# A two-layer encoder trunk: the second dense block's sum and the late gathers put behind the next layer's first two normalisations

## Chip, cores, metric

One core of a Trainium2 chip. The metric is the device time of one execution in microseconds, median of three runs.

## What is computed

512 tokens of width 1024 pass two layers. A layer normalises and modulates, mixes (three kinds of attention, one projection in and one out), adds and normalises, and then sums for every token the 128 experts that its router chose out of 16384 (8 heads, 16 each). The cut that matters:

```python
x = _layer_norm(DEEPNORM_ALPHA * x + (1.0 + g1) * mix, ln1_g[l], ln1_b[l])
h = _modulate(x, sh2, sc2)
u = jnp.take(u_tab, eb, axis=0)
act = jax.nn.gelu(jnp.einsum('tkd,td->tk', u, hb), approximate=False)
vv = jnp.take(v_tab, eb, axis=0)
ffn = jnp.einsum('tk,tkd->td', gb * act, vv)
x = _layer_norm(DEEPNORM_ALPHA * x + (1.0 + g2) * ffn, ln2_g[l], ln2_b[l])
```

The next layer reads that x, so its first normalisation of a token block needs the finished sum of the block.

## The kernel before

The tokens are four blocks of 128 rows, xs[0] to xs[3]. The expert sums are done in two ways at the same time. Blocks 1 and 2 (DENSE) are done by matmul against all experts: `dense` runs 128 tiles of 128 experts, and for each it transposes and splits a tile of u, multiplies, and adds a tile of v into four PSUM banks `acc`. Blocks 0 and 3 are done by gathers: `experts` is a generator with one step for each gathered tile, 32 of u and then 32 of v in turn, 512 steps in all. A step has an indirect DMA on GpSimd's queue into one of the four buffers of `g`, and one VectorE instruction on it: a dot product for u (line 691), a weighted sum for v (line 706). So a buffer of `g` is used again only when VectorE has taken the gather that was in it.

`pace(ex, mark, n)` draws n steps of that generator and ties their VectorE instructions behind the instruction `mark`. Most steps are drawn beside the dense tiles. In layer 0 the last 50 (LATE[0]) are drawn when layer 1 has opened its pools (`late()`), with the mark at the end of block 1's `finish`. These are the last 18 u-gathers and the last 32 v-gathers of block 3, and `finish` of block 3 stands behind them. In layer 1 nothing is late (LATE[1] is 0).

`finish` (line 716) ends a block: it multiplies the sum by the gate row, adds alpha times x (line 718), and normalises into xs (`moments`, `affine`). The rows (gate, gain, bias) are spread over the partitions by a small matmul into a PSUM bank (`row_op`, line 220), in two halves, and VectorE reads the bank (lines 223 and 225). The two dense blocks take those banks from `ut()`, a pair of buffers in the dense loop's own pool. Block 0's and block 3's `finish` take them from `psx`, a pool with one buffer (tile name prow, tag ex). A sum of the dense blocks is copied by ScalarE from PSUM to a tile `fa` in the dense loop's SBUF pool.

Layer 1 begins with `open_attention`, whose pools lie where the dense loop's pools were: what is first written there waits until the dense loop's last use. `layer_setup` then loads small vectors over SyncE's queue, and `prepare` (line 351) normalises xs[0] and xs[1] into `ytok` (line 246), transposes and modulates them into hT. `project` multiplies both with w_in (line 154), `attend` and `output` do block 0, `between` adds and normalises, `queries` does the router's matmul. The order on each engine comes from a scheduler that works from priorities and a simulated timeline, so a change in program order can move instructions that the diff doesn't name.

Of the kernel before, what the change touches and what calls it, by code (L numbers as in the profile page):

```python
# [11 lines left out]
F32 = mybir.dt.float32  # L12
# [5 lines left out]
OP = mybir.AluOpType  # L18
# [3 lines left out]
P = 128  # L22
D = 1024
# [13 lines left out]
LATE = (50, 0)  # L37
# [15 lines left out]
def body(ctx, tc, x, c, positions, ada_w, ada_b, w_in, q_norm_g, kv_norm_g, w_uq, w_ukv, conv_w,  # L53
         w_o, ln1_g, ln1_b, peer_wq, peer_k1, peer_k2, peer_u, peer_v, ln2_g, ln2_b, out):
    nc = tc.nc
# [4 lines left out]
    pw = ctx.enter_context(tc.tile_pool(name="pw", bufs=1))  # L60
    gath = ctx.enter_context(tc.tile_pool(name="gath", bufs=4))
# [181 lines left out]

    def normalize(dst, src):
        mean, r = moments(src)
        nc.vector.tensor_scalar(dst, src, mean, r, op0=OP.subtract, op1=OP.mult)

    def affine(y, dst, tmp, src, ig, ib, mk=None, pool=None):
        mean, r = moments(src, pool)
# [101 lines left out]
    def prepare(y, b):  # L351
        hT = A.work.tile([P, KT, P], F32, name="hT", bufs=2)
        yt = A.work.tile([P, D], F32, name="ytok", bufs=1)
        normalize(yt, xs[b])
        transpose_cols(hT, yt, KT, scale=y.sc1, bias=y.sh1)
        y.hT[b] = hT

    def project(y, blocks, behind=None):
        l = y.l
# [313 lines left out]
    def experts(y, b, eidx, gw):  # L673
        def after(inst):
            if gate[0] is not None:
                tc.add_manual_dep(inst.ins, gate[0].ins.name,
                                  mybir.DependencyInfo(mybir.DependencyClass.NoSync, mybir.DependencyReason.DATA),
                                  reason="expert sums in pace with the dense tiles")

        h2 = pw.tile([P, D], F32, name="h2")  # L680
        nc.sync.dma_start(h2, h2tok[y.l][b // 2])
        acc = pw.tile([P, D], F32, name="acc")
        dots = pw.tile([P, PH, TOPK], F32, name="dots", bufs=1)
        wts = pw.tile([P, PH, TOPK], F32, name="wts", bufs=1)
        for h0 in range(0, PH, HB):
            slots = [(h, k) for h in range(h0, h0 + HB) for k in range(TOPK)]
            for j, (h, k) in enumerate(slots):
                g = gath.tile([P, D], F32, name="g")
                nc.gpsimd.indirect_dma_start(out=g, out_offset=None, in_=u_flat,  # L689
                                             in_offset=bass.IndirectOffsetOnAxis(ap=eidx[:, h, k:k + 1], axis=0))  # L690
                after(nc.vector.scalar_tensor_tensor(out=g, in0=g, scalar=1.0, in1=h2, op0=OP.mult, op1=OP.mult,  # L691
                                                     accum_out=dots[:, h, k:k + 1]))
                yield
            hs = slice(h0, h0 + HB)
            ge = nc.scalar.activation(wts[:, hs, :], dots[:, hs, :], AF.Gelu)
            if b == 0 and h0 < 2:
                exp_ln(ge)
            nc.vector.tensor_tensor(wts[:, hs, :], wts[:, hs, :], gw[:, hs, :], op=OP.mult)
            for j, (h, k) in enumerate(slots):
                g = gath.tile([P, D], F32, name="g")  # L700
                nc.gpsimd.indirect_dma_start(out=g, out_offset=None, in_=v_flat,  # L701
                                             in_offset=bass.IndirectOffsetOnAxis(ap=eidx[:, h, k:k + 1], axis=0))
                if h == 0 and k == 0:
                    r = nc.vector.tensor_scalar(acc, g, wts[:, h, k:k + 1], None, op0=OP.mult)
                else:
                    r = nc.vector.scalar_tensor_tensor(out=acc, in0=g, scalar=wts[:, h, k:k + 1], in1=acc,  # L706
                                                       op0=OP.mult, op1=OP.add)
                after(r)
                if h < PH - 1 or k < TOPK - 1:
                    yield  # L710
        tc.cur_priority -= 1000000
        finish(y, b, acc, lambda: psx.tile([P, 512], F32, name="prow", tag="ex"), pw)
        tc.cur_priority += 1000000
        yield
# [9 lines left out]
    def dense(y, blocks, res):  # L724
# [148 lines left out]
                yield held[0]  # L873
        fas = []
        for i in range(2):
            fa = dw.tile([P, D], F32, name="fa", tag="v", bufs=2)
            for g in range(2):
                nc.scalar.copy(fa[:, g * 512:(g + 1) * 512], acc[i][g])
            fas.append(fa)
        for b, fa in zip(blocks, fas):  # L880
            r = finish(y, b, fa, ut, dw)
            if b == min(blocks):
                held[0] = r
        st.close()
        yield held[0]

    def pace(ex, mark, n):
        gate[0] = mark
        for _ in range(n):
            next(ex)  # L890

    ada_first(range(4))
    for l in range(L):
        if l:
            open_attention(l)
            late()
        y = layer_setup(l)

        def pick(b, v1, fi):
            return topk(l, v1, fi, b, b not in DENSE)  # L900

        res = [None] * NB
        for b in (0, 1):
            prepare(y, b)
        layer_keys(y)
        ps = project(y, (0, 1))
        if l + 1 < L:
            ada_side(0, range(4, 12))
        layer_rows(y)
        behind = None  # L910
        for p in ps:
            b = p[0]
            attend(y, *p)
            if b == 1:
                for b2 in (2, 3):
                    prepare(y, b2)
            h = between(y, b, output(y, b, p[2]))
            r = queries(y, *h, range(4))
            if b == 0:
                behind = r  # L920
            res[b] = pick(b, *h[1:])
        p2, p3 = project(y, (2, 3), behind)
        if l + 1 < L:
            ada_side(1, range(12))
        attend(y, *p2)
        h = between(y, 2, output(y, 2, p2[2]))
        queries(y, *h, range(2))
        attend(y, *p3)
        rt = output(y, 3, p3[2])
        queries(y, *h, range(2, 4))  # L930
        res[2] = pick(2, *h[1:])
        h = between(y, 3, rt, lambda: A.ps.tile([P, 512], F32, name="prow", tag="at", bufs=2))
        queries(y, *h, range(4))
        res[3] = partial(pick, 3, *h[1:])
        A.stack.close()
        dn = dense(y, DENSE, res)
        ex = chain.from_iterable(experts(y, b, *res[b]) for b in range(NB) if b not in DENSE)
        pace(ex, None, EARLY[l])
        groups = 2 * P // TG
        for _ in range(groups):  # L940
            mark = next(dn)
            pace(ex, mark, 1)
        with tc.issue_after(mark.ins):
            res[3] = res[3]()
        n = 2 * 2 * NSLOT - EARLY[l] - LATE[l] - groups
        for a, mark in enumerate(dn):
            if a < NK:
                pace(ex, mark, (a + 1) * n // NK - a * n // NK)
        late = partial(pace, ex, mark, LATE[l])
        if not l + 1 < L:  # L950
            late()


_INS = ["x", "c", "positions", "ada_w", "ada_b", "w_in", "q_norm_g", "kv_norm_g", "w_uq", "w_ukv", "conv_w",
# [19 lines left out]
```

## Time and profile before

| | us |
|---|---|
| median of three runs (lowest, highest) | 3543.99 (3531.81, 3545.16) |
| the profiled execution | 3547.72 |
| its span, first to last instruction | 3546.0 |
| TensorE busy in the span | 3074.8 (87%) |
| VectorE | 2754.8 (78%) |
| GpSimd | 1456.3 (41%) |
| ScalarE | 928.7 (26%) |

Layer 0 ends and layer 1 begins at about 1770 to 1820 us of the span. Times of the rows below are from the span's start. A busy share is an average over stages with different limits, so the stretches around the change are read one by one.

### The profile page before, as it was taken

The page shows a single profiled execution, that of the slowest core. Times are in us where ns is not written, and L with a number is a line of the kernel's source. Part 1 is how long each engine was busy: PE and PEld are TensorE (multiplying, and loading weights), DVE is VectorE, ACT ScalarE, POOL GpSimd, SP SyncE. Part 2 cuts the span into 40 slices and gives each one's busy share as a digit, 9 for nine tenths or more (in the row PEclk, how much of TensorE's full clock was granted, in tenths as well). Part 3 has the DMA queues.
Part 4 walks back from the last instruction along what each step waited for, and adds up shares of the span by engine and source line. Part 5 has one row for each costly group of instructions (what it writes and reads, how often), then busy time and mean ns, then how long its engine had stood idle before and what let it go on. Part 6 is the DMA issues. An engine that isn't in the chain of part 4 may idle for free.

```text
span 3546.0 us, 51872 instructions
## 1 busy us (share of the span) xinstructions
PE 3074.8 (87%) x18364; PEld 2019.4 (57%) x18364; DVE 2754.8 (78%) x6213; ACT 928.7 (26%) x1859; POOL 1456.3 (41%) x1347
## 2 busy tenths in 40 slices
PE   7878879659999999999948987785789999999998
PEld 2433434436777777777724444444567767677775
DVE  3667897999777877677675578889998887776777
ACT  2342432222222222222222223312222222222221
POOL 1034563256433434444451144534454444434443
PEclk9989989859999999999969997896799999999998
DMA  8767968558888888899885577794779988889997
GB/s 290 239 206 256 329 227 305 173 192 289 301 325 304 314 308 320 305 343 350 330 296 198 171 273 259 261 325 155 245 275 344 338 309 318 314 323 335 361 352 255
DMA packets 340051, 1011.98 MB, mean 285 GB/s; under 512 B 40504, under 2 KB 53064, under 8 KB 339792
## 3 DMA queue, kind: packets, MB, share of 16 engines
q0 software_dynamic: 147456, 536.94, 42.5%
q1 hardware_dynamic: 192336, 471.73, 38.2%
q8 instruction: 146, 2.39, 0.3%
q14 instruction: 113, 0.93, 0.1%
HBM read 1002.06 MB, written 6.34 MB: 284 GB/s over the span
## 4 chain that ended last, share of the span: by engine, by line
PE 15%; DVE 12%; DMA 10%; issue 9%; POOL 3%; ACT 1%; DVEq 0%; POOLq 0%; ACTq 0%
DMA g<-in_peer_v,eidx 5%; PE acc L842 4%; PE pm L154 3%; DMA g<-in_peer_u,eidx 3%; DVE g L691 2%; DVE acc L706 2%; POOL g L689 2%; PE sp L824 1%; PE sp L825 1%; PE sp L826 1%; DVE tk_ef L661 1%; PE utp L810 1%; POOL g L701 1%; DVE o L790 1%; DVE o L781 1%
## 5 line engine op out<-in xcount | busy, mean ns | idle before, releaser
L701 POOL DMA_INDIRECT g<-in_peer_v,eidx x512 | 613.7, 1199 | 802.2 <-DVE acc L706 486.4
L842 PE MATMUL acc<-v,ge 128*128 128x512 f32 x2048 | 927.1, 595 | 6.8 <-DVE ge L830 6.7
L689 POOL DMA_INDIRECT g<-in_peer_u,eidx x512 | 593.0, 1158 | 755.8 <-DVE g L691 508.5
L706 DVE SCALAR_TENSOR_TENSOR acc<-g,wts,acc 128x1024 f32<-128x1024 f32 x508 | 668.8, 1316 | 143.0 <-DMA g<-in_peer_v,eidx 139.6
L691 DVE SCALAR_TENSOR_TENSOR g<-g,h 128x1024 f32<-128x1024 f32 x512 | 619.7, 1225 | 180.8 <-DMA g<-in_peer_u,eidx 180.2
L824 PE MATMUL sp<-hh,uh 128*128 128x256 f32 x2048 | 613.7, 300 | 1.1 <-ACT ge L828 1.1
L826 PE MATMUL sp<-hh,ul 128*128 128x256 f32 x2048 | 595.0, 291 | 0.0
L825 PE MATMUL sp<-hl,uh 128*128 128x256 f32 x2048 | 584.5, 285 | 0.0
L842 PEld LDWEIGHTS acc<-v,ge 128*128 128x128 f32 x2048 | 370.1, 190 | 372.0 <-issue 364.3
L812 ACT CAST uh<-utp 128x512 fp32r<-128x512 f32 x512 | 303.3, 594 | 911.7 <-PE utp L810 772.6
L814 DVE TENSOR_TENSOR ul<-utp,uh 128x512 fp32r<-128x512 f32 x512 | 346.5, 684 | 106.9 <-ACT uh L812 106.4
L824 PEld LDWEIGHTS sp<-hh,uh 128*128 128x128 f32 x2048 | 392.9, 192 | 6.1 <-issue 4.1
L825 PEld LDWEIGHTS sp<-hl,uh 128*128 128x128 f32 x2048 | 393.1, 192 | 4.6 <-issue 4.5
L826 PEld LDWEIGHTS sp<-hh,ul 128*128 128x128 f32 x2048 | 391.9, 191 | 0.1
L810 PE MATMUL utp<-ident,u 128*128 128x128 f32 x2048 | 304.9, 278 | 57.0 <-DVE ul L814 54.0
L810 PEld LDWEIGHTS utp<-ident,u 128*128 128x128 f32 x2048 | 237.4, 142 | 136.0 <-issue 66.4
L799 ACT COPY G<-pg 128x344 f32<-128x344 f32 (+1 forms) x192 | 146.4, 763 | 561.8 <-PE pg L797 557.9
L797 PE MATMUL pg<-o,o 128*128 128x43 bf16 (+1 forms) x4608 | 182.5, 190 | 97.7 <-DVE o L790 85.4
L797 PEld LDWEIGHTS <-o 128*128 128x128 bf16 x4608 | 162.6, 102 | 179.9 <-issue 84.5
L154 PE MATMUL pm<-wt,hT 128*128 128x512 f32 (+1 forms) x512 | 231.3, 601 | 24.2 <-DMA wt<-in_w_in 13.4
L154 PE MATMUL pm<-wt,h2T 128*128 128x512 f32 x512 | 238.2, 611 | 8.8 <-DMA wt<-in_peer_wq 8.2
L660 POOL TENSOR_TENSOR tk_pick<-tk_hot,tk_ce 128x400 f32<-128x400 bf16 x128 | 125.7, 982 | 153.6 <-DVE tk_hot L658 151.7
(234 smaller groups left out, 3259.9 us busy)
## 6 DMA issues: line engine op xcount, KB each, us to landing
u<-in_peer_u SPq DMA_DIRECT2D x256, 512.0 KB
v<-in_peer_v SPq DMA_DIRECT2D x256, 512.0 KB
wt<-in_peer_wq SPq DMA_DIRECT2D x128, 512.0 KB
adw<-in_ada_w SPq DMA_DIRECT2D x160, 256.0 KB
wt<-in_w_o SPq DMA_DIRECT2D x64, 512.0 KB
wt<-in_w_in SPq DMA_DIRECT2D x48, 512.0 KB
wt<-in_ada_w SPq DMA_DIRECT2D x16, 512.0 KB
g<-in_peer_u,eidx POOLq DMA_INDIRECT x512, 7.0
```

Of the source, the lines that this page charges most:

```text
L154: r = nc.tensor.matmul(pm[:, :n], lhsT=lhsT[:, k0 + k, :], rhs=wt[:, k, :n], start=k0 + k == 0, stop=k0 + k == KT - 1)
L689: nc.gpsimd.indirect_dma_start(out=g, out_offset=None, in_=u_flat, in_offset=bass.IndirectOffsetOnAxis(ap=eidx[:, h, k:k + 1], axis=0))
L691: after(nc.vector.scalar_tensor_tensor(out=g, in0=g, scalar=1.0, in1=h2, op0=OP.mult, op1=OP.mult, accum_out=dots[:, h, k:k + 1]))
L701: nc.gpsimd.indirect_dma_start(out=g, out_offset=None, in_=v_flat, in_offset=bass.IndirectOffsetOnAxis(ap=eidx[:, h, k:k + 1], axis=0))
L706: r = nc.vector.scalar_tensor_tensor(out=acc, in0=g, scalar=wts[:, h, k:k + 1], in1=acc, op0=OP.mult, op1=OP.add)
L797: nc.tensor.matmul(pg[:, tt, 0:n], lhsT=o2[:, tt // TI, :, tt % TI], rhs=o1a[:, tt // TI, p, 0:n, tt % TI], start=tt == 0 and p == 0, stop ...
L810: nc.tensor.transpose(pt[:, j * P:(j + 1) * P], u[:, k * P:(k + 1) * P], ident)
L814: nc.vector.tensor_tensor(ul.rearrange("p j t -> p (j t)"), pt, uh.rearrange("p j t -> p (j t)").bitcast(F32), op=OP.subtract)
L824: nc.tensor.matmul(sp, lhsT=uh[:, j, :], rhs=hh[:, k, :], start=k == 0, stop=False)
L825: nc.tensor.matmul(sp, lhsT=uh[:, j, :], rhs=hl[:, k, :], start=False, stop=False)
L826: nc.tensor.matmul(sp, lhsT=ul[:, j, :], rhs=hh[:, k, :], start=False, stop=k == KT - 1)
L842: nc.tensor.matmul(acc[i][g], lhsT=w[:, i * P:(i + 1) * P], rhs=v[:, g * 512:(g + 1) * 512], start=a == 0, stop=a == NK - 1)
```

## The change

`dense` finishes only block 1. Block 2's `fa` is put into a buffer of the gathers' ring (tag g), and its `finish` becomes a call that is made later, with the one-buffer pool `psx` and the small tiles of `pw` in place of the dense loop's own. In layer 1's beginning the order of the program is now: prepare blocks 0 and 1, finish block 2 of layer 0, draw the 50 late steps with the mark at block 1's normalisation (the instruction that writes `ytok`). At the end of layer 1 the same call is made after the last dense tile, and `pace` draws none.

```diff
     def prepare(y, b):
...
-        normalize(yt, xs[b])
+        r = normalize(yt, xs[b])
...
+        return r
...
         fas = []
         for i in range(2):
-            fa = dw.tile([P, D], F32, name="fa", tag="v", bufs=2)
+            if i:
+                fa = gath.tile([P, D], F32, name="fa", tag="g")
+            else:
+                fa = dw.tile([P, D], F32, name="fa", tag="v", bufs=2)
...
-        for b, fa in zip(blocks, fas):
-            r = finish(y, b, fa, ut, dw)
-            if b == min(blocks):
-                held[0] = r
+        held[0] = finish(y, blocks[0], fas[0], ut, dw)
+        rest.append(lambda: finish(y, blocks[1], fas[1], lambda: psx.tile([P, 512], F32, name="prow", tag="ex"), pw))
...
         if l:
             open_attention(l)
-            late()
...
         for b in (0, 1):
-            prepare(y, b)
+            r = prepare(y, b)
+        if l:
+            rest.pop()()
+            pace(ex, r, LATE[l - 1])
...
-        late = partial(pace, ex, mark, LATE[l])
         if not l + 1 < L:
-            late()
+            pace(ex, mark, LATE[l])
+            rest.pop()()
```

The order on the engines, at three places. In the names xs_95 to xs_98 are blocks 0 to 3, `g,dots<-g,h` is a u-gather's product, `acc<-g,wts,acc` a v-gather's, utp is a bank of the dense loop's pair, prow one of the pool with one buffer.

VectorE where layer 0 ends, from the end of block 1 to the first write of `ytok`, before:

```order
L225 SCALAR_TENSOR_TENSOR xs_96<-fa,rs_r,utp 128x512 x2
L691 SCALAR_TENSOR_TENSOR g,dots<-g,h_10865 128x1024 x4
L223 TENSOR_TENSOR fa<-fa,utp 128x512 x2
L691 SCALAR_TENSOR_TENSOR g,dots<-g,h_10865 128x1024
L718 SCALAR_TENSOR_TENSOR fa<-xs_97,fa 128x1024
...
L225 SCALAR_TENSOR_TENSOR xs_97<-fa,rs_r,utp 128x512 x2
L691 SCALAR_TENSOR_TENSOR g,dots<-g,h_10865 128x1024 x2
L298 MEMSET sqT 128x1024
...
L691 SCALAR_TENSOR_TENSOR g,dots<-g,h_10865 128x1024
L246 TENSOR_SCALAR ytok<-xs_95,bnmv,rs_r 128x1024
```

and with the change:

```order
L225 SCALAR_TENSOR_TENSOR xs_96<-fa,rs_r,utp 128x512
L225 SCALAR_TENSOR_TENSOR fa<-fa,bnmv,prow 128x512
L225 SCALAR_TENSOR_TENSOR xs_96<-fa,rs_r,utp 128x512
L225 SCALAR_TENSOR_TENSOR fa<-fa,bnmv,prow 128x512
L298 MEMSET sqT 128x1024
...
L225 SCALAR_TENSOR_TENSOR xs_97<-fa,rs_r,prow 128x512
L246 TENSOR_SCALAR ytok<-xs_95,bnmv,rs_r 128x1024
L246 TENSOR_SCALAR ytok<-xs_96,bnmv,rs_r 128x1024
L692 SCALAR_TENSOR_TENSOR g,dots<-g,h_10865 128x1024 x3
L325 CAST rows_160<-rf 32x256
```

Block 2's `finish` runs between block 1's instructions, and the 18 u-products that stood before `ytok` now stand behind it. On GpSimd's queue the first gather that is not yet issued then now stands behind the small instructions of both normalisations and the nine that make the masks; on SyncE's queue no row moves.

VectorE in layer 1's attention of block 0, from the last `ktok` of the projection to the masked scores `sbe`, before:

```order
L477 COPY ktok<-kr 128x8x32
L223 TENSOR_TENSOR acc<-acc,prow 128x512
L718 SCALAR_TENSOR_TENSOR acc<-xs_98,acc 128x1024
L237 BN_STATS bnst<-acc 128x6 x2
L499 TENSOR_REDUCE mx<-sc 128x4
...
L539 SCALAR_TENSOR_TENSOR sp_17102<-z,sbe 128x512
L541 SCALAR_TENSOR_TENSOR sp_17102<-ntri,sp_17102 128x512
L548 SCALAR_TENSOR_TENSOR sbe<-ntri,z 128x512
```

and with the change:

```order
L478 COPY ktok<-kr 128x8x32
L707 SCALAR_TENSOR_TENSOR acc<-g,wts,acc 128x1024
L500 TENSOR_REDUCE mx<-sc 128x4
L707 SCALAR_TENSOR_TENSOR acc<-g,wts,acc 128x1024
L500 TENSOR_REDUCE mx<-sc 128x4
...
L540 SCALAR_TENSOR_TENSOR sp_17102<-z,sbe 128x512
L707 SCALAR_TENSOR_TENSOR acc<-g,wts,acc 128x1024
L542 SCALAR_TENSOR_TENSOR sp_17102<-ntri,sp_17102 128x512
L707 SCALAR_TENSOR_TENSOR acc<-g,wts,acc 128x1024 x5
L549 SCALAR_TENSOR_TENSOR sbe<-ntri,z 128x512
L707 SCALAR_TENSOR_TENSOR acc<-g,wts,acc 128x1024
```

Block 3's `finish` stood here; now 17 v-products stand between the attention's own instructions (16 of them before `sbe`), and the `finish` comes behind them, beside `between` of block 0.

VectorE at the program's end, before (first fence) and with the change (second):

```order
L239 BN_AGGR bnmv<-bnst 128x2
L223 TENSOR_TENSOR fa<-fa,utp 128x512
L225 SCALAR_TENSOR_TENSOR acc<-acc,bnmv,prow 128x512
L223 TENSOR_TENSOR fa<-fa,utp 128x512
L718 SCALAR_TENSOR_TENSOR fa<-xs_97,fa 128x1024
L225 SCALAR_TENSOR_TENSOR acc<-acc,bnmv,prow 128x512
L237 BN_STATS bnst<-fa 128x6 x2
L225 SCALAR_TENSOR_TENSOR xs_98<-acc,rs_r,prow 128x512
```

```order
L239 BN_AGGR bnmv<-bnst 128x2
L225 SCALAR_TENSOR_TENSOR acc<-acc,bnmv,prow 128x512 x2
L225 SCALAR_TENSOR_TENSOR xs_98<-acc,rs_r,prow 128x512 x2
L223 TENSOR_TENSOR fa<-fa,prow 128x512 x2
L719 SCALAR_TENSOR_TENSOR fa<-xs_97,fa 128x1024
L237 BN_STATS bnst<-fa 128x6 x2
L239 BN_AGGR bnmv<-bnst 128x2
L225 SCALAR_TENSOR_TENSOR fa<-fa,bnmv,prow 128x512 x2
L225 SCALAR_TENSOR_TENSOR xs_97<-fa,rs_r,prow 128x512 x2
```

Blocks 3 and 2 took turns there, with banks of their own; now block 2 follows block 3, and both use the one prow bank.

## Rows read from the trace of the kernel before

**Rows 1.** The page: its span, and the group of the v-gathers' products

```profile
span 3546.0 us, 51872 instructions
...
L706 DVE SCALAR_TENSOR_TENSOR acc<-g,wts,acc 128x1024 f32<-128x1024 f32 x508 | 668.8, 1316 | 143.0 <-DMA g<-in_peer_v,eidx 139.6
```

**Rows 2.** Busy time by stretch: end of layer 0, start of layer 1, the program's end

```profile
core 0: us, PE busy (x) PEld busy (x) DVE busy (x) ACT busy (x) POOL busy (x), PEclk, DMA share, GB/s
1771.00:1803.00 32.00, 7.92 (x27) 3.13 (x25) 27.27 (x46) 2.25 (x4) 18.45 (x18) 0.58 0.64 215
1803.00:1822.00 19.00, 1.94 (x9) 1.60 (x9) 14.60 (x26) 8.62 (x12) 14.14 (x21) 0.50 0.95 283
1822.00:1912.00 90.00, 76.99 (x226) 37.82 (x227) 53.88 (x101) 24.42 (x67) 34.04 (x30) 0.92 0.86 309
1912.00:1966.00 54.00, 43.50 (x225) 28.77 (x224) 31.35 (x56) 19.99 (x60) 4.07 (x10) 0.88 0.26 84
3518.00:3546.00 28.00, 11.27 (x37) 4.58 (x35) 23.37 (x34) 2.24 (x4) 3.21 (x6) 0.60 0.23 92
```

**Rows 3.** Timeline of VectorE, 1774 to 1820: start, us, instruction, idle before and releaser

```profile
1774.14 1.22 DVE L718 SCALAR_TENSOR_TENSOR fa<-xs,fa 128x1024 f32<-128x1024 f32 x1
...
1777.05 1.41 DVE L225 SCALAR_TENSOR_TENSOR fa<-fa,bnmv,utp 128x512 f32<-128x512 f32 x2
1778.53 1.41 DVE L225 SCALAR_TENSOR_TENSOR xs<-fa,rs_r,utp 128x512 f32<-128x512 f32 x2
...
1801.88 1.40 DVE L225 SCALAR_TENSOR_TENSOR xs<-fa,rs_r,utp 128x512 f32<-128x512 f32 x2
...
1816.40 0.81 DVE L246 TENSOR_SCALAR ytok<-xs,bnmv,rs_r 128x1024 f32<-128x1024 f32 x1 [2.12 <-POOL rs_r L230]
...
1819.39 0.81 DVE L246 TENSOR_SCALAR ytok<-xs,bnmv,rs_r 128x1024 f32<-128x1024 f32 x1 [2.08 <-PE pt L258]
```

**Rows 4.** Timeline of TensorE, the first work of layer 1

```profile
1817.36 1.94 PE L258 MATMUL pt<-ident,ytok 128*128 128x128 f32 x8 [18.16 <-DVE wts L698]
1822.00 5.64 PE L154 MATMUL pm<-wt,hT 128*128 128x416 f32 x8 [2.70 <-DMA wt<-in_w_in]
```

**Rows 5.** Timeline of SyncE's queue, layer 1's first load and its first w_in loads

```profile
1803.40 0.38 SPq L287 DMA_DIRECT2D sc<-mod  x1
...
1810.54 5.07 SPq L151 DMA_DIRECT2D wt<-in_w_in  x4
```

**Rows 6.** u-gathers (line 689), 1780 to 1805: issue to landing

```profile
DMA to landing us min/median/max: 5.4/5.5/5.8
```

**Rows 7.** v-gathers (line 701), 1845 to 1870: issue to landing

```profile
DMA to landing us min/median/max: 6.9/6.9/7.1
```

**Rows 8.** Timeline of VectorE, layer 1's attention of block 0

```profile
1910.66 0.29 DVE L477 COPY ktok<-kr 128x256 f32<-128x256 f32 x1 [0.59 <-PE pt L474]
...
1914.83 0.69 DVE L499 TENSOR_REDUCE mx<-sc 128x4 f32<-128x512 f32 x1 [0.47 <-PE sc L497]
...
1932.21 0.69 DVE L548 SCALAR_TENSOR_TENSOR sbe<-ntri,z 128x512 f32<-128x512 f32 x1 [4.39 <-PE z L544]
...
1947.61 1.28 DVE L223 TENSOR_TENSOR rt<-rt,prow 128x512 f32<-128x512 f32 x2
```

**Rows 9.** The chain that ended last, 1766 to 2010: start, us, what

```profile
1929.63 5.54 DMA wt<-in_w_o
```

**Rows 10.** Timeline of VectorE, the program's end

```profile
3532.60 0.69 DVE L223 TENSOR_TENSOR fa<-fa,utp 128x512 f32<-128x512 f32 x1
...
3535.72 0.74 DVE L225 SCALAR_TENSOR_TENSOR acc<-acc,bnmv,prow 128x512 f32<-128x512 f32 x1
...
3537.57 0.73 DVE L225 SCALAR_TENSOR_TENSOR xs<-acc,rs_r,prow 128x512 f32<-128x512 f32 x1
...
3540.44 1.40 DVE L225 SCALAR_TENSOR_TENSOR xs<-fa,rs_r,utp 128x512 f32<-128x512 f32 x2
```

**Rows 11.** Timeline of TensorE, the program's end: one fill of the prow bank

```profile
3536.52 0.58 PE L220 MATMUL prow<-rows,sel 96*128 96x256 bf16 x2 [1.34 <-DVE acc L225]
```

More of the change, by code (lines that the diff above doesn't have):

```diff
@@ L245, in normalize @@
         mean, r = moments(src)
-        nc.vector.tensor_scalar(dst, src, mean, r, op0=OP.subtract, op1=OP.mult)
+        return nc.vector.tensor_scalar(dst, src, mean, r, op0=OP.subtract, op1=OP.mult)
     def affine(y, dst, tmp, src, ig, ib, mk=None, pool=None):
@@ L687, in experts @@
             for j, (h, k) in enumerate(slots):
-                g = gath.tile([P, D], F32, name="g")
+                g = gath.tile([P, D], F32, name="g", tag="g")
                 nc.gpsimd.indirect_dma_start(out=g, out_offset=None, in_=u_flat,
@@ L699, in experts @@
             for j, (h, k) in enumerate(slots):
-                g = gath.tile([P, D], F32, name="g")
+                g = gath.tile([P, D], F32, name="g", tag="g")
                 nc.gpsimd.indirect_dma_start(out=g, out_offset=None, in_=v_flat,
@@ L879, in dense @@
             fas.append(fa)
-        for b, fa in zip(blocks, fas):
-            r = finish(y, b, fa, ut, dw)
-            if b == min(blocks):
-                held[0] = r
+        held[0] = finish(y, blocks[0], fas[0], ut, dw)
+        rest.append(lambda: finish(y, blocks[1], fas[1], lambda: psx.tile([P, 512], F32, name="prow", tag="ex"), pw))
         st.close()
         yield held[0]
+    rest = []
     def pace(ex, mark, n):
```

## The prediction

> **What bounds the kernel now.** I read the page first, then the busy time by stretch, then the timelines of single engines around the change, and last the chain of waits. The page gives the span, 3546.0 us [rows 1]. The profiled execution took 3547.7 us, 3.7 above the median of the runs (0.1%). My sum is made against 3547.7, and the median is forecast by the same difference. A measurement of this kernel can tell about 0.5% from no change, 17.7 us.
>
> By stretch [rows 2], the dense loop leaves TensorE almost no gap, but the seam between the layers does. From 1771 to 1822, 51 us, TensorE is busy for under 10 us at a granted clock of 0.58 and then 0.50, while VectorE is busy for 27 of the first 32 us. So VectorE's order sets the length of the seam. From 1822 to 1912 (the projection) TensorE is busy for 77 of 90 us and the DMA engines for 0.86. From 1912 to 1966 (attention of block 0) TensorE has 43.5 of 54 us, in short pieces of a chain of dependent steps, and the DMA share falls to 0.26. The last 28 us are VectorE again.
>
> In the seam [rows 3] block 1's finish begins with the line 718 at 1774.14 and ends at 1778.53 + 1.41 = 1779.94. Block 2's ends at 1801.88 + 1.40 = 1803.28, because 18 products of late gathers stand before the two ytok, most of them before 1803. The ytok are written at 1816.40 and 1819.39. SyncE's first load of layer 1 goes out at 1803.40, right when block 2 leaves the dense pool, and its first w_in load at 1810.54 [rows 5]. TensorE begins the projection at 1822.00, 11.5 after that load's issue [rows 4].
>
> **The change, part by part.**
>
> *The seam.* Block 1's finish now has block 2's instructions between its own: by the new order some 3.5 us of work, where VectorE had waited for none. It ends at about 1783.4 and block 2's, outside the pool, at about 1790.5. The pool is free 1803.28 - 1783.4 = 19.9 us earlier, so SyncE's loads move by 19.9. That is the low end of the gain: the projection starts 11.5 us behind its load as before. The high end is the ytok. Without the 18 products (about 1.3 us each, 23 us) it comes when block 2's last half and the GpSimd power are done, at about 1791, 25.4 earlier; the first matmul is 1822.00 - 1816.40 = 5.6 behind the first ytok [rows 3, 4]. The loads meet only a few gathers now, where the DMA share was 0.95 [rows 2], so I take a value near the high end: **-24** (bounds -20 and -25.4).
>
> *The late gathers in the projection.* The ring of four holds block 2's fa until 1790.5, so three gathers are issued ahead, and the fourth waits for that and for the masks on GpSimd's queue. They then meet the projection in the same order as before: up to the second ktok 33 products now stand where 32 stood. One product more: **+1** (bounds 0 and +2: one v-product takes 1.316 [rows 1], and one period of the ring is at most 2.1, below).
>
> *The late gathers in the attention.* The other 17 now stand in VectorE's order among the attention's own instructions, and ScalarE and TensorE wait for those. Before, from the first mx at 1914.83 to sbe at 1932.21 it took 17.4 us [rows 8]. Now 15 products stand between these two. A buffer of the ring comes round after landing, product and hand-over, 5.5 + 1.3 + 0.1 = 6.9 us where the DMA engines are not full [rows 6], so one gather in 1.73 us; where they are, 6.9 + 1.4 = 8.3, one in 2.08 [rows 7]. Fifteen at 1.73 and one mx are 26.6 us, 9.2 more than before; at 2.08, 14.5 more. If none were waited for, 15 x 1.316 [rows 1] and 5.2 us of the attention's own work (seven instructions of 0.69 [rows 8] and two small ones) give 24.9, 7.5 more. The DMA share of the stretch was 0.26, so I take 9. But TensorE was not ready behind sbe: the chain shows it waiting 5.5 us for w_o there [rows 9]. Those loads go out when earlier weights are used, which the longer attention delays less than it delays sbe. So of 9 us some 4 arrive at rt (1947.61 before [rows 8]): **+4** (bounds +2 and +14.5).
>
> [...]
>
> *Block 3's finish.* It stood beside the attention where VectorE waited anyway. Now it follows the last product and runs into between of block 0: two halves at 0.69 [rows 10], line 718 to the first affine half 2.9 (1777.05 - 1774.14), four affine halves at 0.7 [rows 3], together 7.1. Part is done before rt arrives: **+4** (bounds 0 and +7.1). Its reader is the second projection, behind all queries of block 0, so nobody else is late.
>
> *The end of layer 1.* Before, block 3 and block 2 took turns, and the last half was read at 3540.44 + 1.40 = 3541.84 [rows 10]. Now block 3's four affine halves begin at 3532.60, in the place of fa, and block 2 follows through the same single bank. One hand-over of that bank is 3537.57 - 3535.72 = 1.85 us [rows 10]: VectorE's 0.74, TensorE's fill 0.58 [rows 11], and the rest semaphores. Five hand-overs (three more halves of block 3, two of block 2) bring 3532.60 to 3541.85; its second half and the middle of finish take 0.69 + 2.9; three more hand-overs 5.55, the last half 0.74: 3551.7. The loss is 3551.7 - 3541.8: **+9.9** (bounds +4, if halves overlap, and +12).
>
> *At nothing:* the smaller ring while fa is in it (the late gathers stand still then anyway), ScalarE's gelu weights a few places later (they are not read before the v-products), and small moves among the dense tiles of layer 1, where TensorE is the bound.
>
> Sum: -24 + 1 + 4 + 4 + 9.9 = **-5**, so 3542.5 for this execution, and for the median 3544 - 5 = **3539 us**. The seam's gain is given back in three places.
>
> **Rivals.**
>
> *The gain stays (faster).* If the loads run freely in the seam, the projection also loses its later waits for weights. TensorE has 13 idle us in its 90 [rows 2]; about 4 of them would go. With the attention at +2, block 3's finish at 0 and the end at +7: -25.4 - 4 + 1 + 2 + 7 = -19, 3525 us. For it: the DMA share of 0.95 and 0.86 [rows 2]. Against it: the end's single bank, whose price is measured.
>
> *The attention becomes gather-paced (slower).* If gathers land in 6.9 us there and nothing covers it, the attention costs +14.5, block 3's finish +7, and TensorE's pieces get gaps. [...] If the 43.5 busy us of that stretch fall from 0.88 to 0.7, they take 11 us more. With the gain at its low end: -20 + 1 + 14.5 + 7 + 11 + 9.9 = +23, 3567 us. It decides where a gather's period in the attention is above 2 us and the clock falls there. Against it: the share of 0.26. [...]
>
> *The change does nothing at the seam.* If the new pools were released by something else than block 1, the -24 would be small. With -5 there the sum is +14, 3558. The order speaks against it, since both ytok stand before every late product.
>
> **How the numbers follow.** My sum 0.67, the gain that stays 0.18, the gather-paced attention 0.10, no effect at the seam 0.05. Of my own case nearly all lies within 17.7 us: its bounds as a worst sum are -25.4 + 2 + 0 + 4 = -19 and -20 + 2 + 14.5 + 7.1 + 12 = +16. So faster by over 0.5% 0.19, within it 0.70, slower 0.11. The range must hold the sum's bounds and part of both rivals: 3520 to 3557.
>
> **What would show it.** Right: the first w_in matmul at 1796 to 1802; ytok at about 1791; sbe later behind ktok than 21.6 us, by some 9; rt to the last h2d half longer by some 4; at the end eight readings of prow in a row, 1.85 us apart, and a last half some 10 us behind the last dense copy's old distance. Wrong: a first matmul after 1805; w_in loads not moved; an attention without waits for g; an end where blocks 3 and 2 still overlap; a granted clock under 0.8 from 1890 to 1950.

## The result, and the profile after

The changed kernel takes 3513.0 us (median of 7 runs, 3503.61 to 3521.07). In the same session the kernel before took 3543.99. The ratio is 0.9917, 95% interval 0.9898 to 0.9937. The forecast was 3539 with a range down to 3520: the change is faster by 31 us, not by 5, and lies outside the range.

The page of the changed kernel, its span and the group that answers to [rows 1]:

```profile
span 3514.0 us, 51880 instructions
...
L707 DVE SCALAR_TENSOR_TENSOR acc<-g,wts,acc 128x1024 f32<-128x1024 f32 x508 | 670.0, 1319 | 131.2 <-DMA g<-in_peer_v,eidx 125.2
```

Busy time by stretch, with the columns of [rows 2]: the seam from block 1's finish to the first w_in product, the projection, the first 54 us of attention, the program's end.

```profile
1774.70:1797.80 23.10, 9.33 (x36) 4.51 (x34) 19.34 (x33) 10.43 (x15) 10.37 (x20) 0.68 0.57 151
1797.80:1885.50 87.70, 76.97 (x222) 37.35 (x222) 52.54 (x119) 23.74 (x65) 39.55 (x35) 0.93 0.93 333
1885.50:1939.50 54.00, 42.91 (x166) 25.51 (x166) 40.87 (x53) 15.02 (x47) 16.87 (x16) 0.75 0.66 224
...
3480.00:3514.00 34.00, 10.86 (x36) 4.27 (x34) 23.93 (x34) 2.28 (x4) 3.22 (x6) 0.59 0.17 69
```

The seam's DMA share fell from 0.64 and 0.95 to 0.57. The attention's rose from 0.26 to 0.66: that is where the late gathers went. VectorE is busy there for 40.9 of 54 us (31.4 before), and TensorE's granted clock fell from 0.88 to a mean of 0.75: from 1885.5 to 1909 it was 0.50.

Timeline of VectorE in the seam and in the attention, answering to [rows 3, 8]:

```profile
1785.99 0.74 DVE L225 SCALAR_TENSOR_TENSOR xs<-fa,rs_r,utp 128x512 f32<-128x512 f32 x1
...
1792.32 0.75 DVE L225 SCALAR_TENSOR_TENSOR xs<-fa,rs_r,prow 128x512 f32<-128x512 f32 x1 [0.49 <-PE prow L220]
1792.98 0.81 DVE L246 TENSOR_SCALAR ytok<-xs,bnmv,rs_r 128x1024 f32<-128x1024 f32 x1
...
1885.48 0.29 DVE L478 COPY ktok<-kr 128x256 f32<-128x256 f32 x1 [1.18 <-PE pt L475]
...
1920.13 0.68 DVE L549 SCALAR_TENSOR_TENSOR sbe<-ntri,z 128x512 f32<-128x512 f32 x1
...
1932.07 1.28 DVE L223 TENSOR_TENSOR rt<-rt,prow 128x512 f32<-128x512 f32 x2
```

SyncE's first load of layer 1 and its w_in loads, then TensorE's first product of layer 1, answering to [rows 5] and [rows 4]:

```profile
1786.86 0.38 SPq L287 DMA_DIRECT2D sc<-mod  x1
...
1791.32 2.93 SPq L151 DMA_DIRECT2D wt<-in_w_in  x4
```

```profile
1797.76 1.73 PE L154 MATMUL pm<-wt,hT 128*128 128x416 f32 x2 [1.89 <-DMA wt<-in_w_in]
```

The first product is 24.2 us earlier, the second ktok 25.2, sbe 12.1, rt 15.5. Layer 0 has the same order in both kernels, but this execution reached the seam 3.7 us later: the last group of layer 0's dense products starts at 1770.28, at 1766.60 before. The table below therefore counts from the start of that group, which it calls the dense end.

The program's end on VectorE: the halves read from the single bank prow, answering to [rows 10].

```profile
3494.16 0.75 DVE L225 SCALAR_TENSOR_TENSOR acc<-acc,bnmv,prow 128x512 f32<-128x512 f32 x1
3495.62 0.75 DVE L225 SCALAR_TENSOR_TENSOR acc<-acc,bnmv,prow 128x512 f32<-128x512 f32 x1 [0.70 <-PE prow L220]
3497.10 0.75 DVE L225 SCALAR_TENSOR_TENSOR xs<-acc,rs_r,prow 128x512 f32<-128x512 f32 x1 [0.73 <-PE prow L220]
...
3509.32 0.75 DVE L225 SCALAR_TENSOR_TENSOR xs<-fa,rs_r,prow 128x512 f32<-128x512 f32 x1 [0.68 <-PE prow L220]
```

Ten halves go through the one bank, as forecast: six in a row and, behind the middle of block 2's finish, four more. In a row they are 1.42 to 1.48 us apart and not 1.85.

This table looks for the 31 us: the length in us of each stage in one profiled execution, from the starts and ends of named instructions, for the two kernels and six of the experiments. A point u n is the start of the n-th copy uh of layer 1's dense rows, counted from 0; an expert tile has two of them, and what the expectations call tile n is u n. The end is the end of VectorE's last half.

| stage | before | end only | before, 51 late | before, picks | after | end before | end before, 51 late | end before, picks |
|---|---|---|---|---|---|---|---|---|
| dense end to first w_in product | 55.4 | 55.5 | 55.9 | 57.0 | 27.5 | 27.5 | 27.5 | 27.4 |
| to the end of the second pair's first 32 w_in products | 196.5 | 196.8 | 199.9 | 197.2 | 207.8 | 202.1 | 213.7 | 213.8 |
| to the last router scores | 385.0 | 384.1 | 380.2 | 388.1 | 376.6 | 380.1 | 381.8 | 383.0 |
| to u 8 | 131.9 | 131.4 | 129.1 | 137.3 | 128.9 | 134.7 | 129.9 | 132.4 |
| u 8 to u 40 | 143.2 | 142.3 | 137.3 | 130.6 | 133.5 | 134.4 | 140.4 | 130.5 |
| u 40 to u 184 | 574.3 | 575.8 | 576.1 | 561.7 | 570.2 | 570.3 | 577.9 | 562.3 |
| to the last dense product | 268.1 | 268.5 | 267.7 | 267.7 | 267.7 | 268.6 | 268.6 | 268.2 |
| to the end | 20.9 | 27.3 | 20.8 | 20.5 | 27.6 | 21.1 | 20.6 | 20.6 |

Before against after: the seam -27.9, the projection, the attention and what follows up to the second projection +11.3, the end +6.7. Those three were forecast as -24, +9 and +9.9. The rest, some 25 us, comes from stages that the forecast had at nothing: -8.4 up to the router's scores, -3.0 to u 8, -9.7 from u 8 to u 40, -4.1 behind it. (Together that is 35 us; the 3.7 us by which this execution was late at the seam come off.) The diff names no instruction in those stages. But VectorE's order is another one there: the scheduler, which sets the order by its own clock, wrote the second pair's attention and the dense rows anew when the seam moved.

### The profile page after: what moved, and what is told of

Read it like the earlier page. It is cut to its first block, busy times and chain, and to the rows that moved or that the text cites. A ratio compares the mean times of both kernels' runs of the same rounds, so it can differ in the third digit from the quotient of the medians.

```text
span 3514.0 us, 51880 instructions
## 1 busy us (share of the span) xinstructions
PE 3083.3 (88%) x18364; PEld 2018.6 (57%) x18364; DVE 2749.9 (78%) x6213; ACT 929.0 (26%) x1859; POOL 1444.3 (41%) x1347
## 4 chain that ended last, share of the span: by engine, by line
PE 30%; DVE 27%; DMA 19%; issue 16%; POOL 5%; ACT 1%; SPq 0%; POOLq 0%; DVEq 0%; ACTq 0%
DMA g<-in_peer_v,eidx 9%; PE acc L843 8%; PE pm L154 7%; DMA g<-in_peer_u,eidx 5%; DVE g L692 4%; DVE acc L707 4%; DMA adw<-in_ada_w 3%; DVE tk_ef L662 3%; POOL g L690 3%; PE sp L825 2%; PE sp L826 2%; PE sp L827 2%; DVE o L791 2%; PE utp L811 2%; DVE o L782 2%
```

## The experiments

**The end, undone and alone.** The first kernel is the changed one with layer 1's end as before (its edit is shown); the second is the kernel before with the new end only. On VectorE each keeps its parent's order up to the end.

```diff
-            if i:
+            if i and l + 1 < L:
...
-        rest.append(lambda: finish(y, blocks[1], fas[1], ...psx..., pw))
+        if l + 1 < L:
+            rest.append(lambda: finish(y, blocks[1], fas[1], ...psx..., pw))
+        else:
+            finish(y, blocks[1], fas[1], ut, dw)
...
-            rest.pop()()
```

> The changed kernel, but layer 1 ends as before: both dense blocks of layer 1 are finished between the dense rows and the last late gathers, with their own buffers. Seam and middle of layer 1 keep the changed kernel's order of instructions on every engine. Theory (the changed kernel won its time at the seam and in the middle of layer 1 and pays at the end for the single bank): about 7 us under the changed kernel, 3506 us, and the last xs half 26 to 32 us after the last dense matmul instead of the changed kernel's 25.9 us plus nothing for the finish behind it. Rival A (the end itself brought a gain, because the late gathers' sums no longer wait for block 2's finish): about 5 to 25 us over the changed kernel. Rival B (the end is neutral): 3513 +- 3 us.

> The kernel before with the end of layer 1 alone changed: block 2's finish behind the last late gathers, through the one bank, its input in the gather ring. Seam and middle of layer 1 keep the order of the kernel before on every engine. Theory: 7 to 10 us slower than the kernel before (ratio 1.002 to 1.003), and layer 1's dense stage as long as in the kernel before. Rival A (the end brings the unexplained gain): 15 to 30 us faster. Rival B (the end is neutral): ratio 1.000.

Measured: ratio 0.9905 (0.9883 to 0.9928) and 1.0009 (0.9992 to 1.0025). In the traces the new end costs 6.5 and 6.4 us (27.6 against 21.1, 27.3 against 20.9); the totals agree with that but can't tell it from nothing. The last half stands 24.8 us behind the start of the last group of dense products, a little under what was expected. So the end brought none of the gain. The table also shows how far two executions of one order differ: up to 1.5 us a stage between before and end only, up to 6 between after and end before.

**Each half of the seam alone.** One kernel moves only the late gathers, the other only block 2's finish; both keep the old end.

```diff
-            if i:
+            if False:
...
-        rest.append(lambda: finish(y, blocks[1], fas[1], ...psx..., pw))
+        finish(y, blocks[1], fas[1], ut, dw)
...
         if l:
-            rest.pop()()
             pace(ex, r, LATE[l - 1])
...
```

```diff
         if l:
             open_attention(l)
+            late()
...
             rest.pop()()
-            pace(ex, r, LATE[l - 1])
...
```

> The changed kernel with both dense blocks finished at the seam and at the end as before; only the late gathers stand behind the next layer's first two normalisations. At the seam one finish (about 7 us of VectorE) stands ahead of the first normalisation again, so the first w_in matmul comes about 7 us later than in the changed kernel and about 17 us earlier than in the kernel before; the order in the middle of layer 1 is a third one. Theory 1 (the 25 us beyond the prediction came from the order in which the dense stage of layer 1 was written out, which any shift of the seam draws anew): the middle of layer 1, from the first matmul of the last two blocks' projection to the end of the dense rows, has a length of its own, anywhere from 1480 to 1520 us, not tied to the seam's gain. Theory 2 (it came from the late gathers leaving the seam, so that the gather queue and the weight loads meet less): the middle is as short as in the changed kernel, 1486 +- 6 us, and the total about 3505 to 3515 us.

> The changed kernel with the late gathers at the seam where they were, before the first normalisation; only block 2's finish stands behind the normalisations. Layer 1's end as before. The late gathers' sums stand ahead of the first normalisation again, so the first w_in matmul comes within 8 us of the kernel before's distance to the dense end. Theory 1 (order drawn anew): the middle of layer 1 has a length of its own, anywhere from 1480 to 1520 us. Theory 2 (the late gathers' move gives the middle's gain): the middle is as long as in the kernel before, 1512 +- 6 us, and the total 3530 to 3550 us.

Measured: 0.9911 (0.9885 to 0.9936) and 0.9915 (0.9892 to 0.9938): as far as the totals can tell, either half alone gives the whole gain. SyncE's first load of layer 1, first with the late gathers moved alone, then with the finish moved alone:

```profile
1787.65 0.38 SPq L287 DMA_DIRECT2D sc<-mod  x1
```

```profile
1785.25 0.38 SPq L287 DMA_DIRECT2D sc<-mod  x1
```

The first w_in product comes 31.6 and 28.7 us behind the dense end (27.5 in the changed kernel, 55.4 before). Only the two together were expensive: in the order before, block 2's finish stands among products that wait for gathers, and layer 1's first load goes out when that finish has left the dense pool. The distance expected for the finish alone was wrong by some 19 us. Both kernels have the changed kernel's VectorE order in the dense rows, so they could not tell whether the order or the seam makes the middle shorter. The middle, as the expectations count it, took 1510 and 1499 us, where theory 2 wanted about 1486 and 1512; but the changed kernel took 1489 and the same with the old end 1500, so one trace of each decides little.

**The order without the seam, the seam without the order.** One late gather more (51 for 50) makes the scheduler write the dense rows otherwise. In the traces the kernel before then has the changed kernel's VectorE order in the dense rows, but for one pair of one-hots ahead of u 8. (The expectation counts the second pair's attention in; there the two traces differ in some 45 places.) The changed kernel (with the old end) then has exactly the order of the kernel before in its dense rows. That is a crossed pair for one line, as far as the dense rows go.

```diff
-LATE = (50, 0)
+LATE = (51, 0)
```

> The kernel before with 51 late gathers instead of 50 and nothing else. The seam keeps its form (both finishes and the late sums ahead of the first normalisation), but the scheduler then writes VectorE's work from layer 1's second pair of blocks to the end of the dense rows in exactly the changed kernel's order. Theory (the order of VectorE's work, not the earlier seam, makes the middle of layer 1 shorter): from the first matmul of the dense products to w_in of layer 1 about 55 us as before; tiles 8 to 40 of layer 1's dense rows take 134 to 136 us where the kernel before takes 142 to 143; the GpSimd products tk_pick take about 0.92 us where they took 1.21; the total 8 to 15 us under the kernel before (ratio 0.996 to 0.998). Rival (the middle is shorter because layer 1 starts earlier against the gathers and weight loads): tiles 8 to 40 stay at 142 to 143 us and the ratio is 1.000 to 1.001.

> The changed kernel with layer 1's end as before, and 51 late gathers instead of 50. The seam is the changed kernel's; VectorE's work in layer 1's dense rows is then written in exactly the order of the kernel before. Theory (order): tiles 8 to 40 take 142 to 143 us instead of 134 to 135, tk_pick 1.21 us, the total 5 to 12 us over the same kernel with 50 late gathers: ratio 0.993 to 0.995 against the kernel before. Rival (the earlier seam makes it): tiles 8 to 40 stay at 134 to 135 us, ratio 0.990 to 0.991.

Measured: 0.9982 (0.9963 to 1.0001) and 0.9956 (0.9941 to 0.9971). Busy time from u 8 to u 40 (columns of [rows 2]) of before, of before with 51, of after, and of the old end with 51:

```profile
2535.40:2678.60 143.20, 127.41 (x917) 92.85 (x917) 133.99 (x242) 35.83 (x66) 73.78 (x65) 0.98 0.83 291
```

```profile
2527.20:2664.50 137.30, 125.33 (x918) 91.82 (x917) 128.77 (x240) 35.47 (x65) 71.53 (x64) 0.99 0.86 301
```

```profile
2511.10:2644.60 133.50, 124.50 (x915) 91.29 (x914) 126.71 (x237) 35.16 (x66) 70.30 (x64) 0.99 0.87 301
```

```profile
2521.60:2662.00 140.40, 127.84 (x918) 93.83 (x917) 133.73 (x242) 35.48 (x66) 70.98 (x65) 0.96 0.84 297
```

The length goes with the order, not with the seam, by 6 of the 8 us expected; VectorE is busy for 134 us in the one order and for 127 to 129 in the other. It holds in all traces of the two orders: three with the order of the kernel before take 140.4 to 143.2 us, six with the changed kernel's 133.3 to 137.3. So it is VectorE more than TensorE that sets the length of this stretch. The totals say less: the interval of the first kernel reaches 1.

**Why one order is slower.** In this stretch VectorE builds G, the gate weights of the dense rows, from one-hots (`o<-iotab,i2T` and a second one) and bf16 products with the gates (`o<-o,gT`), and GpSimd makes tk_pick, a product by which block 3's experts are looked up. Costly groups from u 8 to u 40 (busy us, mean ns of one). Before, VectorE's sums of u-gathers, the bf16 product and the one-hot for G, and GpSimd's tk_pick:

```profile
L691 DVE SCALAR_TENSOR_TENSOR g<-g,h 128x1024 f32<-128x1024 f32 x17 | 21.4, 1282 | 2.7 <-DMA g<-in_peer_u,eidx 2.7
...
L790 DVE TENSOR_TENSOR o<-o,gT 128x336 bf16<-128x336 bf16 x39 | 13.2, 388 | 0.0
L781 DVE TENSOR_TENSOR o<-iotab,i2T 128x1024 bf16<-128x1024 bf16 x13 | 10.9, 837 | 0.1
...
L660 POOL TENSOR_TENSOR tk_pick<-tk_hot,tk_ce 128x400 f32<-128x400 bf16 x16 | 19.3, 1207 | 7.5 <-DVE tk_hot L658 7.2
```

The same of after:

```profile
L692 DVE SCALAR_TENSOR_TENSOR g<-g,h 128x1024 f32<-128x1024 f32 x15 | 18.1, 1219 | 2.7 <-DMA g<-in_peer_u,eidx 2.7
...
L791 DVE TENSOR_TENSOR o<-o,gT 128x336 bf16<-128x336 bf16 x39 | 11.7, 344 | 0.0
L782 DVE TENSOR_TENSOR o<-iotab,i2T 128x1024 bf16<-128x1024 bf16 x12 | 9.1, 761 | 0.0
...
L661 POOL TENSOR_TENSOR tk_pick<-tk_hot,tk_ce 128x400 f32<-128x400 bf16 x16 | 14.8, 924 | 4.0 <-DVE tk_hot L659 3.6
```

The groups with 51 late gathers, tk_pick of before and then of the old end, have the mean of the order they carry:

```profile
L660 POOL TENSOR_TENSOR tk_pick<-tk_hot,tk_ce 128x400 f32<-128x400 bf16 x16 | 14.8, 925 | 4.0 <-DVE tk_hot L658 3.6
```

```profile
L661 POOL TENSOR_TENSOR tk_pick<-tk_hot,tk_ce 128x400 f32<-128x400 bf16 x16 | 19.3, 1208 | 7.4 <-DVE tk_hot L659 7.2
```

Timeline of the kernel before, VectorE and then GpSimd, shows one such meeting:

```profile
2592.52 1.69 DVE L781 TENSOR_TENSOR o<-iotab,i2T 128x1024 bf16<-128x1024 bf16 x1
...
2595.85 0.68 DVE L814 TENSOR_TENSOR ul<-utp,uh 128x512 fp32r<-128x512 f32 x1
2596.45 2.04 DVE L790 TENSOR_TENSOR o<-o,gT 128x336 bf16<-128x336 bf16 x3
```

```profile
2592.77 0.88 POOL L660 TENSOR_TENSOR tk_pick<-tk_hot,tk_ce 128x400 f32<-128x400 bf16 x1
...
2596.93 0.88 POOL L660 TENSOR_TENSOR tk_pick<-tk_hot,tk_ce 128x400 f32<-128x400 bf16 x1
```

Away from a tk_pick the one-hot takes 0.68 us and three o<-o,gT 0.81. Here, beside one, they take 1.69 and 2.04: 1.01 and 1.23 more, where the GpSimd product takes 0.88. At 2602.57 and 2574.33 it is GpSimd that is slow, 2.97 and 2.98 us for a product of 0.88 beside a row of VectorE's, and the one-hot in each of those rows keeps 0.68. The kernel before has two one-hots and two triples that are held up like this in the stretch, the changed kernel one one-hot and a triple that is 0.67 us too long. (The six and five of the expectation below are means of groups.) The f32 sums are held up too: six before take 1.65 to 2.31 us where others take 1.2 to 1.3, and four after take 1.55 to 2.09. Put together, 12 VectorE instructions of the stretch run over the median of their like by 0.1 us or more, 9.7 us in all; with the change it is 9, by 5.3 us. The crossed pair follows the order: 5.3 us in the kernel before with 51, 10.0 in the old end with 51. In all fourteen traces every such instruction overlaps a tk_pick. So some 4.4 of the 7.3 us that VectorE is busy for less are meetings of this kind. The other 3 us are work that has left the stretch: two u-sums (17 and 15 in the rows above) and one one-hot that stand elsewhere in the changed order.

Not all VectorE work is held up there: of the ul<-utp,uh, which read utp from a PSUM bank, four overlap a tk_pick in the stretch before and take 0.67 to 0.69 us, where the 28 others take 0.63 to 0.69; after, six overlap one and take 0.67 to 0.68. Nor did the first to begin win here: by the record the one-hot began 0.25 us before the tk_pick and was still the one held up. By what rule one of the two engines is held up was not shown.

To try this cause by itself, block 3's tk_pick go to VectorE, 16 in each layer, in the kernel before and in the changed one with the old end. Those two have the same VectorE order in the dense rows.

```diff
-                nc.gpsimd.tensor_tensor(pick, hot, ce...)
+                (nc.vector if b == 3 else nc.gpsimd).tensor_tensor(pick, hot, ce...)
```

> The kernel before with the products tk_pick of block 3 (16 in each layer) on VectorE instead of GpSimd. Theory (in tiles 8 to 40 of layer 1 the builds' products and one-hots stand beside GpSimd's tk_pick, and the two engines hold each other up): no o<-o,gT or o<-iotab,i2T takes over 0.35 or 0.75 us any more in that stretch (six took 0.68 and five 1.08 in the kernel before); what that saves, about 5 us, VectorE pays back with 16 products of 0.4 to 0.9 us each, so tiles 8 to 40 take 138 to 148 us and the total stays within 0.3% of the kernel before. Rival (the long ones were long for another reason, such as their place behind a one-hot): the same number of them stays long.

> The changed kernel with layer 1's end as before, and block 3's tk_pick on VectorE. VectorE's order in layer 1's dense rows is the same as that of the kernel before with tk_pick on VectorE, only the seam and the attention of layer 1 differ, so the two give what the seam alone is worth. Theory: 15 us (12 to 20) between the two, as the prediction's seam sum has it without the end. Rival (the changed kernel's whole gain comes with the seam, whatever the order): 26 to 33 us between the two.

Measured: 0.9929 (0.9903 to 0.9955) and 0.9867 (0.9842 to 0.9892). The first kernel's groups from u 8 to u 40:

```profile
L691 DVE SCALAR_TENSOR_TENSOR g<-g,h 128x1024 f32<-128x1024 f32 x12 | 14.5, 1229 | 3.9 <-DMA g<-in_peer_u,eidx 3.9
...
L790 DVE TENSOR_TENSOR o<-o,gT 128x336 bf16<-128x336 bf16 x39 | 11.0, 343 | 0.0
L660 DVE TENSOR_TENSOR tk_pick<-tk_hot,tk_ce 128x400 f32<-128x400 bf16 x16 | 9.4, 587 | 0.0
L781 DVE TENSOR_TENSOR o<-iotab,i2T 128x1024 bf16<-128x1024 bf16 x12 | 8.4, 696 | 0.0
```

None of those products is long any more: the longest one-hot takes 0.75 us and the longest o<-o,gT 0.39 (0.35 had been set as the most), and no VectorE instruction of the stretch runs over its like by 0.1 us. So the meetings are gone, and with them the 9.7 us that they cost the kernel before. What that is worth is not read from the length. The stretch takes 130.6 and 130.5 us, under the 138 to 148 expected, but 9.4 us of tk_pick came to VectorE, and 7 us of u-sums went out of the stretch (12 in place of 17 in the rows), most of them to behind u 40, where VectorE is busy for about 80% of the time. The expectation had not reckoned with those. The total falls by 0.7% where 0.3% was the most, and where the rest of that lies was not settled: u 40 to u 184 is 12.6 and 8.0 us shorter than in the parents, but the six traces with the changed kernel's order differ there by 13.5 us (564.8 to 578.3); and layer 0's last group of dense products starts at 1760.5 and 1762.4 in these two traces, between 1760.8 and 1774.6 in the other twelve.

The pair gives the seam for one order: 0.9929 - 0.9867 = 0.0062, 22 us of 3551 (with an uncertainty of 13), between what the two theories expected and so for neither.

**Other orders.** The number of sums ahead of layer 1's dense rows, 110, is changed to 112 in the kernel before, and to 112 and 108 in the changed one with the old end. The last kernel has 40 late gathers.

```diff
-EARLY = (80, 110)
+EARLY = (80, 112)
```

> The kernel before with 112 instead of 110 expert sums issued ahead of layer 1's dense rows. Seam and attention of layer 1 keep their order; the dense rows get a third order. Theory (order): tiles 0 to 40 take another time than in either kernel, by 3 us or more (they took 251 us in the kernel before, 242 in the changed one), and the total moves with them, to either side. Rival: two sums more of 512 change nothing that can be measured, 251 +- 2 us and ratio 1.000.

> The changed kernel with layer 1's end as before and 112 instead of 110 sums ahead of layer 1's dense rows: another order there. Theory (the order's part and the seam's part add): the total lies between the one with the order of the kernel before and the one with the changed kernel's, 3508 to 3528 us at 3542 for the kernel before. If it lies under 3505, the better order of the two is not the best one.

> The changed kernel with layer 1's end as before and 108 instead of 110 sums ahead of layer 1's dense rows: a fourth order there. Theory: as for 112, 3508 to 3528 us at 3542 for the kernel before; tiles 8 to 40 take 133 to 143 us, and the more of the builds stand beside GpSimd's tk_pick, the longer.

> The changed kernel with layer 1's end as before, and 40 late gathers instead of 50: ten more stand among the dense rows of layer 0. From the second pair of blocks on, VectorE's order is the changed kernel's. Theory (the late gathers that stand behind the normalisations are paid in layer 1's first attention): the stretch from the first products of layer 1's first projection to the end of the second pair's projection is 4 to 10 us shorter than with 50 (187.5 us in its run), and layer 0's dense rows are 0 to 8 us longer, so that the total lies within 5 us of the one with 50. Rival (that stretch is bound by TensorE and its clock, not by the late sums): it keeps 185 to 190 us.

Measured: 0.9965 (0.9951 to 0.9979), 0.9920 (0.9895 to 0.9944), 0.9923 (0.9900 to 0.9946) and 0.9910 (0.9885 to 0.9936). Two sums of 512 placed elsewhere make the kernel before 12 us faster, and u 0 to u 40 takes 246 us in place of 251, so the order counts, as the theory had it. The stretch from u 8 to u 40 takes 138.2, 138.2 and 136.8 us in the first three. The meetings alone don't set it: VectorE's instructions run over by 6.9, 5.2 and 8.5 us there, and in the second kernel VectorE is busy for 126 us, as in the changed kernel, and waits 11 us for gathers (6 in the changed kernel). With 40 late gathers the stage up to the second pair's w_in takes 199.8 us where 50 took 202.1: 2.3 less, not 4 to 10. One trace of each can't settle that, since two executions of one order differ by 5.7 us in this stage (207.8 and 202.1).

## Why the prediction was wrong

**Right: the seam.** "The projection starts 11.5 us behind its load as before" was its low end, the ytok its high end, and -24 was taken. By the clock of the trace the first product moved by 24.2 us, but this execution reached the seam 3.7 us late. Counted from the dense end, the first load moved by 20.2 us (forecast 19.9), the first ytok by 27.1 (forecast 25.4) and the first product by 27.9, a little beyond the high bound of 25.4: w_in followed the first load in 4.5 us (7.1 before), and the product came 6.4 us behind w_in's issue. That the late sums alone or the finish alone would do was not seen.

**Nearly right in its sum, by luck: what the seam gives back.** The product more in the projection (+1) did not show: the second ktok kept the gain, -25.2, 0.9 better than the first product. The attention cost 13.1 us at sbe (forecast 9) and 9.6 at rt (forecast 4): the wait for w_o hid less than was thought. From the first mx to sbe it took 30.9 us where 26.6 were forecast, 13.5 more than before, close to the 14.5 that the working had for full DMA engines. It chose the lower price by a DMA share of 0.26, which the late gathers themselves then raised, to 0.88 from 1897 to 1909 and 0.96 from 1909 to 1921. Block 3's finish took another 2.2 (the last h2d half stands at 1950.35, at 1963.70 before; forecast 4). Together 10.9 where 9 were forecast, from one term of more than twice its size and two that came out smaller. The granted clock of 0.75 is a sign of the rival with the gather-paced attention, which was given 0.10; its price for the attention came, its total did not. No run shows its 11 us for TensorE at a clock of 0.7 in place of 0.88: from the second ktok to rt TensorE is busy for 37.4 us (126 matmuls) at a mean clock of 0.71, where it was 31.5 us (146) at 0.93 before. The rival in which the gain stays, 3525 with a chance of 0.18, came nearest in the number, but not by its terms: the projection became shorter by 1 us and not by 4, and the attention gave back 9.6 and not 2.

**Mis-sized: the end.** +9.9 was taken, 6.7 came. The hand-over of the bank was priced at 1.85 us from one pair of readings that had other work between them; in a row it takes 1.42 to 1.48. Eight of them at that price give the difference. Beside VectorE's reading of 0.69 to 0.75 and TensorE's fill of 0.58 to 0.61 only 0.08 to 0.15 us is left of a hand-over in a row, and not the 0.53 that was put down to semaphores.

**The step that failed** is the line "At nothing: ... small moves among the dense tiles of layer 1, where TensorE is the bound". TensorE is the bound of the dense rows from u 184 on: it is busy for 267.9 of the last 268.1 us before, and all eight kernels of the table take the same time there to within 0.9 us. From u 8 to u 40 it is VectorE: 134 us of work in 143, and TensorE waited for its ul. The waits of TensorE in that stretch, total us, times, longest, before and then after:

```profile
PE utp L810 <- DVE ul L814: 14.2, 12, 3.8
```

```profile
PE utp L811 <- DVE ul L815: 4.7, 5, 1.6
```

The prediction read the dense loop as one stage, and so a new order there was taken for free. Three pairs of kernels with one VectorE order in the dense rows price the seam without the end: before to old end with 51, 0.0044, 16 us; before with 51 to old end, 0.0077, 27 us; the two with picks, 22 us. Each carries an uncertainty of 5 to 13 us; the forecast had -15. The orders that 51 and 50 late gathers give differ by the rest: 0.0018 with the old seam and 0.0051 with the new one, 6 us (uncertainty 7) and 18 us (uncertainty 10), and the forecast had 0. Not all of that is the dense rows: with 51 the order of the second pair's attention is another one as well.

What stays open: the 3.0 to u 8, the 4.1 behind u 40 and most of the 8.4 us before the router's scores are of a size by which executions of one order differ too, so the cause of some 15 of the 25 us is not shown. Only the stretch u 8 to u 40, 9.7 us, has its cause shown: the order in both directions, and within it the meetings of the two engines, which are gone when tk_pick moves. How much of the loss at sbe is gathers and how much the clock was not tried.

The best kernel tried is the changed one with the old end and block 3's tk_pick on VectorE: 0.9867, 3503.1 us where the kernel before took 3550.9 in that session.

## What to carry to other kernels

Where a scheduler writes the order, an edit at one place draws the order anew at places that the diff does not name: compare the whole order, and ask in each stage whether the engine whose order changed is its bound, by stretches and not by the loop's average. Before a gain is credited to an edit, make one neutral change (one gather more, two sums more) to both kernels and see how far that alone moves the time; here it moved it by up to 0.5%, more than the edit was forecast to bring. And a stretch that has become shorter may only have less work in it: count its instructions before its time is called a gain. When an order matters, look for VectorE work that stands beside GpSimd products: from u 8 to u 40 such work ran over its like by 9.7 us in the kernel before and by 5.3 in the changed one.

## What the runs showed of the hardware that was not expected

In the kernel before, a bf16 one-hot of 0.68 us took 1.69 beside a GpSimd product of 0.88, though it started first, and two GpSimd products of 0.88 took 2.97 and 2.98 us beside a row of VectorE's. From u 8 to u 40 every VectorE instruction that ran over its like by 0.1 us or more, in any of the fourteen traces, overlapped such a product: 12 in the kernel before, 9 in the changed one. On VectorE the same 128x400 product took 0.59 us in the mean, in the kernel before with picks. A hand-over of one PSUM bank, from VectorE's reading through TensorE's fill of 0.58 to 0.61 us to the next reading, took 1.42 to 1.48 us at the end of the changed kernel.
